# Tables of LayerNorm and spatial mixing loaded and turned at the gate, and a longer booking for transposing DMAs in a planned decoder-trunk step

## The chip, the cores and the metric

The kernel runs on one core of one Trainium2 chip. The metric is the device time of one execution in microseconds (us), lower is better. Several executions are timed without the profiler; one more is profiled, and its trace is what the readings below rest on.

## The reference

One layer of a decoder trunk is applied to 1024 prompt rows and 8 sample rows of width 1024, in float32. What matters for this change is the branch A:

```
xn = rmsnorm(h) * pre_g
u, v, z_a, x_b, z_b, g_a, g_b = split(xn @ w_in)          # seven blocks of 1024 columns
u = gelu(u)
vn = layernorm(gelu(v)) * ln_g + ln_b                     # statistics over the 1024 columns of a row
s = tril(w_s[g]) @ vn + b_s[g]                            # 8 groups g of 128 channels, chunks of 128 rows
y_a = u * s * silu(z_a)
...                                                       # branch B: trailing means, block-diagonal product
m = sigmoid(g_a) * (y_a @ w_pa) + sigmoid(g_b) * (y_b @ w_pb)
h = h + rmsnorm(m @ w_out) * post_g
h = h + rmsnorm(sigmoid(rmsnorm(h) @ w_pg) * (p @ w_ple)) * ple_out_g
```

Outputs are the new rows, the normalised v of the last chunk and of the sample rows, and the pooling buffers.

## The kernel before, in words

Float32 accuracy comes from cutting each operand into a high and a low part (`split`: one copy on ScalarE, one subtraction on VectorE) and multiplying three of the four combinations on TensorE. Each block of 1024 output columns is done as four pairs of 128-column tiles. The first pair of v is done classically in four products; every other pair is done after Strassen's scheme in seven products P1, P6, P2, P7, P4, P5, P3 (`strassen`, L632), whose operand quarters of x (B11 to B22, T1 to T4) stay in SBUF, and whose weight combinations (A11, S2, ...) are made on VectorE and cut on both engines a few products ahead. P5 and P3 use one PSUM region: VectorE copies P5's result out before P3 adds to it.

The stream of steps (`run_stream`, L730) goes through v, then the gate g_a, then u and z_a, then branch B, the gate g_b, and the merging products. The raw weights of a pair are asked for six steps ahead (FETCH, L750), and cut three ahead (AHEAD, L32). Work beside the products is hung on steps: `at(step, f)` calls f after that step. A finished pair of v, which has channels on the partitions, is turned to rows: `v_planes` (L871) copies its 16-bit halves to words on ScalarE and has SyncE's queue issue one transposing DMA for each of the two tiles, `v_join` (L880) copies the turned halves to their place on ScalarE, and `v_turn` (L889) applies gelu there. The 8 sample rows of v are turned on TensorE. In the gate's first products the LayerNorm of the rows follows (`ln_stats`, `ln_apply` L917), first that of the samples, whose rows are multiplied and shifted by the tables `lng` and `lnb`; `sample_spatial` (L1001) is their mixing, `spatial_offsets` (L965) and `spatial` that of the prompt.

The tables of the change: `ln_loads` (L936) loads w_s (0.5 MB) and 16 short rows of ln_g and ln_b; `spatial_weights` (L948) masks w_s on GpSimd, turns it in eight 128 by 128 transposes on TensorE, cuts it in two `split`s into the tiles `wst`, and turns the 16 short rows into `lncol`; `ln_rows` (L943) loads ln_g, ln_b and b_s broadcast to all partitions, 0.5 MB each.

The order of instructions is not that of the code. A planner (class `Planner`) records every operation with its engine, its estimated duration, the tiles it touches, and its due time `at`: the time of the TensorE stream at which it was asked for. It then simulates the five engines and emits each engine's instructions in the order of their planned start (`order`, L202). Latest starts are counted back from TensorE's due times (`wanted`, L180). An operation is planned no earlier than 14 us ahead of its latest start or its `at`, whichever comes first (`LOAD`, `LEAD`, L65). Among operations that an engine could start at the same time the one with the earliest latest start goes first; an engine waits for one that is overdue and soon ready, when the other can spare the time (L248). A DMA keeps its queue busy for `op.busy`, then shares one pipe of 0.36 MB per us for `op.moved`, and lands `op.lands` later. Nearly all tiles live in 46 equal slots (SLOTS, L31) that are handed on in the order in which they come free; a load is planned only when three more slots than it needs are free (`SPARE`, L65). On the chip each engine, and SyncE's queue among them, works through its instructions in the planned order, and a semaphore makes it wait where data is later than planned.

```
161:        if method[:9] == "dma_start":
162:            op.busy, op.moved = 1.0 if engine == "gpsimd" else 0.45, writes[0].size() * (2e-6 if writes[0].dtype == U16 else 4e-6)
163:            op.lands = 4.5 if kwargs.get("accum_op") is not None else 2.0
...
1278:    at(c[1], ln_loads)
1279:    at(vsteps[1][2], spatial_weights)
...
1289:    at(vsteps[3][0], ln_rows)
```

`c` is the classical first pair of v, `vsteps[i]` the steps of v's pair i, `gasteps[0]` those of the gate's first pair.

Of the kernel before, what the change touches and what calls it, by code (L numbers as in the profile page):

```python
# [55 lines left out]
class Planner:  # L56
# [89 lines left out]
    def take(self, engine, method, args, kwargs):  # L146
        given = [*(("out" if i == 0 else "", a) for i, a in enumerate(args)), *kwargs.items()]
        writes = [a for k, a in given if k in ("out", "accum_out") and a is not None]
        reads = [a for k, a in given if k not in ("out", "accum_out") and hasattr(a, "tensor")]
        if kwargs.get("accum_op") is not None:  # L150
            reads += writes
        name = writes[0].tensor.name
        if engine == "tensor" and self.open is not None and self.open[0] == name:
            op = self.open[1]
        else:
            op = Op(engine, len(self.ops), self.clock, self.fixed)
            self.ops.append(op)
        self.open = (name, op) if engine == "tensor" else None
        op.calls.append((method, args, kwargs))
        op.spent.append(op.busy)  # L160
        if method[:9] == "dma_start":
            op.busy, op.moved = 1.0 if engine == "gpsimd" else 0.45, writes[0].size() * (2e-6 if writes[0].dtype == U16 else 4e-6)
            op.lands = 4.5 if kwargs.get("accum_op") is not None else 2.0
        else:
            took = self.duration(engine, method, writes[0], reads, kwargs)
            op.busy += took
            if engine == "tensor" and not self.fixed:
                self.clock += took
            if engine == "scalar":
                op.table = self.TABLES.get(kwargs["func"], 0)  # L170
        for ap in reads:
            self.touch(op, ap, False)
        for ap in writes:
            self.touch(op, ap, True)
# [124 lines left out]
@with_exitstack  # L299
def tile_hybrid_step(ctx, tc, *args):  # L300
    hybrid_step(ctx, tc, *args)


def hybrid_step(
# [107 lines left out]
    class Operand:  # L412
# [37 lines left out]
        def at(self, what, k):  # L450
            return [part[:, k % 2, :] for part in self.parts[what, k // 2]]
# [437 lines left out]
    def v_turn(out, pair, ts):  # L889

        if ts == [S]:
            ps = bank("vt")
            for m in range(2):
                nc.tensor.transpose(ps[:NS, m * P : (m + 1) * P], out[m][:, SEQ:T], ident)
        for t in ts:
            n, c = rows(t), slice(2 * pair * P, (2 * pair + 2) * P)
            v = vtok(t)[:n, c]
            nc.scalar.activation(out=v, in_=ps[:NS, : 2 * P] if t == S else v, func=AF.Gelu_apprx_tanh,
                                 accum_out=vsums[:n, t, pair : pair + 1])
# [324 lines left out]
    def pairs_of(c0, cls, key):  # L1224
        return [(Weights(inp(c0, i), key), cls(i, key)) for i in range(NPAIR)]
# [5 lines left out]
    vsteps, vusers = [], []  # L1231
# [3 lines left out]
    gasteps = [strassen(w, xop, u) for w, u in pairs_of(GA0, Gate, "ga")]  # L1235
# [11 lines left out]
    flat, c = big.rearrange("p b t -> p (b t)"), [T + 4 * w for w in (0, HALF, HALF + WIDE, HALF + 2 * WIDE)]  # L1247
# [20 lines left out]
    c = vsteps[0]  # L1268
# [6 lines left out]
    at(vsteps[1][0], lambda: xop.cut("T4"))  # L1275


    at(c[1], ln_loads)
    at(vsteps[1][2], spatial_weights)
    for i, u in enumerate(vusers):  # L1280

        nxt = vsteps[1][1:] + vsteps[2] if i == 0 else (vsteps[i + 1] if i + 1 < NPAIR else gasteps[0])
# [3 lines left out]
            at(nxt[2 + m], lambda u=u, i=i, m=m: v_join(u.out, i, m))  # L1286
        for s, ts in zip(nxt[4:], V.turns):
            at(s, lambda i=i, ts=ts: v_turn(None, i, ts))
    at(vsteps[3][0], ln_rows)
    flow = [s for p in gasteps for s in p] + [s for p in usteps[0] for s in p]  # L1290
    for n, t in enumerate([NB - 1, *range(NB - 1)]):
        s = 5 + 4 * n
# [43 lines left out]
    p, l, c = gbsteps[2], gbsteps[3], pasteps[0]  # L1336
    turn_over(yaop, l, [*l[1:], c[0]])
    p, l, c = pasteps[2], pasteps[3], pbsteps[0]
# [196 lines left out]
    l, c = pbsteps[3], outsteps[0]  # L1535
    turn_over(woop, l, [*l[2:], c[0], c[1]], ("B11", "T3", "T2", "B21", "T4", "T1", "B22"))
    l, c = outsteps[3], gatesteps[0]
# [194 lines left out]
```

## Time and profile before

| | us |
|---|---|
| median of 3 runs | 1000.1 (1000.04 to 1001.04) |
| profiled execution, whole | 997.51 |
| its span, first to last instruction | 995.8 |
| PE (TensorE matmul) busy | 981.3 |
| DVE (VectorE) busy | 800.5 |
| ACT (ScalarE) busy | 526.0 |
| POOL (GpSimd) busy | 72.7 |

The span is what the profile shows from the first to the last instruction; the execution's time has 1.7 us more around it. Busy times of different engines overlap. PE stands for matmuls and PEld for weight loads; SP is SyncE, which only issues DMAs here. Tiles go by the program's names: `vw` is a cut weight or the words of v, `garaw` the gate's raw weights, `gas` their sums, `gaw` their cut parts, `v<-vw` on SP a transposing DMA, `big<-v` on ACT the copy of turned halves, `vt` the turned sample rows of v, `acc` a PSUM region, `u` a Strassen partial sum. A timeline row gives start, length, engine, line, operation, tiles, shapes and count, and in brackets the idle time of the engine before it and what ended it. All operations are recorded by the planner, so they share one line, L297, and are told apart by tiles.

### The profile page before, as it was taken

The page shows a single profiled execution, that of the slowest core. Times are in us where ns is not written, and L with a number is a line of the kernel's source. Part 1 is how long each engine was busy: PE and PEld are TensorE (multiplying, and loading weights), DVE is VectorE, ACT ScalarE, POOL GpSimd, SP SyncE. Part 2 cuts the span into 40 slices and gives each one's busy share as a digit, 9 for nine tenths or more (in the row PEclk, how much of TensorE's full clock was granted, in tenths as well). Part 3 has the DMA queues.
Part 4 walks back from the last instruction along what each step waited for, and adds up shares of the span by engine and source line. Part 5 has one row for each costly group of instructions (what it writes and reads, how often), then busy time and mean ns, then how long its engine had stood idle before and what let it go on. Part 6 is the DMA issues. An engine that isn't in the chain of part 4 may idle for free. (4 is left out here: it accounts for less than half of the span.)

```text
span 995.8 us, 16069 instructions
## 1 busy us (share of the span) xinstructions
PE 981.3 (99%) x6136; PEld 881.0 (88%) x6136; DVE 800.5 (80%) x1241; ACT 526.0 (53%) x925; POOL 72.7 (7%) x162
## 2 busy tenths in 40 slices
PE   8999999999999999999999999999999999999996
PEld 6889989999999899999999999999999988888885
DVE  5975468777778888888897987697799798779796
ACT  7767888756434434243433343562353365677653
POOL 2200000000000000001000100000000002312111
PEclk9999999999999999999999999999999999999999
DMA  9334462232365355546635166874663553389646
GB/s 342 128 124 85 110 169 106 86 107 64 135 230 186 104 184 185 197 134 227 240 120 166 40 238 232 287 287 149 215 254 110 172 206 68 84 275 364 166 108 191
DMA packets 103970, 171.14 MB, mean 172 GB/s; under 512 B 24254, under 2 KB 64238, under 8 KB 103885
## 3 DMA queue, kind: packets, MB, share of 16 engines
q1 hardware_dynamic: 101525, 162.21, 47.9%
q0 software_dynamic: 2048, 7.37, 4.3%
q8 instruction: 48, 0.79, 0.3%
q10 hardware_dynamic: 320, 0.54, 0.2%
q14 instruction: 29, 0.24, 0.1%
HBM read 114.59 MB, written 51.77 MB: 167 GB/s over the span
## 5 line engine op out<-in xcount | busy, mean ns | idle before, releaser
L297 DVE TENSOR_TENSOR u<-acc,u 128x520 f32<-128x520 f32 (+1 forms) x90 | 62.6, 696 | 38.8 <-PE acc L297 36.8
L297 POOL TENSOR_TENSOR rstd<-ms,mhalf 128x1 f32<-128x1 f32 (+1 forms) x45 | 36.5, 812 | 213.6 <-DVE ms L297 213.5
L297 POOL MEMSET u<- 128x8 f32 x35 | 3.5, 105 | 558.1 <-PE acc L297 310.9
L297 ACT ACTIVATE u<-acc 128x512 f32<-128x512 f32 x39 | 23.2, 595 | 26.9 <-PE acc L297 26.4
L297 ACT ACTIVATE paw<-pas 128x512 fp32r<-128x512 f32 x16 | 10.1, 629 | 31.2 <-DVE pas L297 25.9
L297 ACT ACTIVATE pbw<-pbs 128x512 fp32r<-128x512 f32 x16 | 10.0, 630 | 28.2 <-DVE pbs L297 24.9
L297 DVE TENSOR_TENSOR big<-big 128x1024 f32<-128x1024 f32 (+4 forms) x20 | 23.6, 1217 | 0.0
L297 ACT ACTIVATE big<-v 128x1024 uint16<-128x1024 uint16 x16 | 18.5, 1173 | 8.4 <-DMA v<-vw 8.4
L297 ACT ACT_TABLE_LOAD x15 | 19.2, 1283 | 6.5 <-PE acc L297 5.5
L297 ACT ACTIVATE big<-pht,gvec 128x128 f32<-128x128 f32 x64 | 18.0, 381 | 8.1 <-PE pht L297 8.1
L297 ACT ACTIVATE big<-mix 128x256 f32<-128x256 f32 x32 | 12.2, 384 | 16.9 <-PE mix L297 16.2
L297 PE MATMUL accm<-qh,wpoolw 128*128 128x260 f32 (+1 forms) x96 | 20.9, 320 | 0.0
L297 DVE TENSOR_TENSOR acc<-acc,u 128x512 f32<-128x512 f32 (+1 forms) x16 | 11.2, 699 | 8.8 <-PE acc L297 8.8
L297 DVE TENSOR_TENSOR big<-mix,big 128x256 f32<-128x256 f32 x32 | 13.2, 422 | 5.9 <-ACT big L297 5.0
L297 ACT ACTIVATE zbw<-zbs 128x512 fp32r<-128x512 f32 x16 | 10.1, 632 | 14.6 <-DVE zbs L297 7.2
L297 ACT ACTIVATE zaw<-zas 128x512 fp32r<-128x512 f32 x16 | 10.0, 630 | 14.5 <-DVE zas L297 9.0
L297 ACT ACTIVATE gbw<-gbs 128x512 fp32r<-128x512 f32 x16 | 10.0, 626 | 13.9 <-DVE gbs L297 12.0
L297 PEld LDWEIGHTS accm<-qh,wpoolw 128*128 128x128 f32 x96 | 15.5, 188 | 1.9
L297 ACT ACTIVATE zbw<-zbraw 128x512 fp32r<-128x512 f32 x12 | 7.5, 627 | 17.8 <-DMA zbraw<-in_w_in_dram 16.3
L297 ACT ACTIVATE uw<-us 128x512 fp32r<-128x512 f32 x16 | 10.0, 627 | 12.3 <-DVE us L297 9.8
L297 ACT ACTIVATE junk<-ge 128x512 bf16<-128x512 f32 (+2 forms) x19 | 11.6, 609 | 8.9 <-DVE ge L297 8.3
L297 ACT ACTIVATE gb<-gb 128x1032 f32<-128x1032 f32 (+1 forms) x8 | 6.8, 854 | 17.6 <-DVE gb L297 17.6
(689 smaller groups left out, 3632.2 us busy)
## 6 DMA issues: line engine op xcount, KB each, us to landing
ga<-ga SPq DMA_DIRECT2D x16, 516.0 KB
gb<-gb SPq DMA_DIRECT2D x16, 516.0 KB
ya<-za SPq DMA_DIRECT2D x8, 516.0 KB
yb<-zb SPq DMA_DIRECT2D x8, 516.0 KB
x<-in_x_prompt_dram SPq DMA_DIRECT2D x8, 512.0 KB
vraw<-in_w_in_dram SPq DMA_DIRECT2D x8, 512.0 KB
e<-e SPq DMA_DIRECT2D x8, 512.0 KB
garaw<-in_w_in_dram SPq DMA_DIRECT2D x8, 512.0 KB
```

What stands on the lines that cost most here:

```text
L297: getattr(getattr(self.nc, e), method)(*args, **kwargs)
```

## The change

A transposing DMA gets costs of its own in the planner: it keeps its queue for 3.0 us, takes almost nothing of the pipe, and lands 1.5 us later. The loads of w_s and of the short rows are asked for after the fourth product of v's third pair instead of after the second product of all; the turning of these tables, and the broadcast rows of ln_g, ln_b and b_s, after the first product of the gate instead of after the third product of v's second pair and the first product of v's fourth. The functions themselves are unchanged.

```diff
@@ -161,6 +161,8 @@
         if method[:9] == "dma_start":
             op.busy, op.moved = 1.0 if engine == "gpsimd" else 0.45, writes[0].size() * (2e-6 if writes[0].dtype == U16 else 4e-6)
             op.lands = 4.5 if kwargs.get("accum_op") is not None else 2.0
+            if method == "dma_start_transpose":
+                op.busy, op.moved, op.lands = 3.0, 0.01, 1.5
         else:
             took = self.duration(engine, method, writes[0], reads, kwargs)
             op.busy += took
@@ -1275,8 +1277,8 @@
     at(vsteps[1][0], lambda: xop.cut("T4"))
 
 
-    at(c[1], ln_loads)
-    at(vsteps[1][2], spatial_weights)
+    at(vsteps[2][3], ln_loads)
+    at(gasteps[0][0], spatial_weights)
     for i, u in enumerate(vusers):
 
         nxt = vsteps[1][1:] + vsteps[2] if i == 0 else (vsteps[i + 1] if i + 1 < NPAIR else gasteps[0])
@@ -1286,7 +1288,7 @@
             at(nxt[2 + m], lambda u=u, i=i, m=m: v_join(u.out, i, m))
         for s, ts in zip(nxt[4:], V.turns):
             at(s, lambda i=i, ts=ts: v_turn(None, i, ts))
-    at(vsteps[3][0], ln_rows)
+    at(gasteps[0][0], ln_rows)
     flow = [s for p in gasteps for s in p] + [s for p in usteps[0] for s in p]
     for n, t in enumerate([NB - 1, *range(NB - 1)]):
         s = 5 + 4 * n
```

## The prediction

> **What bounds the kernel now.** I read the busy time by stretches first, because the page gives PE 99% of the span and the question is where the last per cent sits.
>
> ```profile
> core 0 of [0], span 995.8 us
> core 0: us, PE busy (x) PEld busy (x) DVE busy (x) ACT busy (x) POOL busy (x), PEclk, DMA share, GB/s
> 0.00:25.00 25.00, 20.79 (x116) 17.16 (x117) 14.00 (x28) 19.05 (x31) 7.04 (x29) 1.00 0.99 348
> 75.00:100.00 25.00, 25.00 (x173) 22.98 (x172) 14.68 (x24) 18.03 (x27) 0.00 (x0) 1.00 0.48 86
> 125.00:135.00 10.00, 8.14 (x53) 6.80 (x53) 7.79 (x13) 7.96 (x18) 0.00 (x0) 1.00 0.68 199
> 135.00:165.00 30.00, 30.00 (x204) 27.62 (x203) 22.94 (x47) 28.26 (x60) 2.38 (x5) 1.00 0.45 112
> 320.00:330.00 10.00, 9.47 (x68) 8.76 (x67) 9.93 (x17) 5.38 (x11) 0.11 (x1) 1.00 0.17 51
> 980.00:995.80 15.80, 7.87 (x46) 6.72 (x44) 10.02 (x20) 5.86 (x15) 2.42 (x3) 0.87 0.77 233
> sum 995.80, PE 981.27 PEld 880.98 DVE 800.49 ACT 525.97 POOL 72.70; mean PE 98.13 PEld 88.10 DVE 80.05 ACT 52.60 POOL 7.27
> ```
>
> PE is idle for 995.80 − 981.27 = 14.53 us: 4.21 in the start, 7.93 in the tail, 1.86 between 125 and 135, 0.53 between 320 and 330. These four add up to 14.53, so PE has no other idle time. Start and tail lie outside the edits; what can be won lies at 125 to 135, where the last pair of v ends and the gates begin. Second, PE's timeline there (start, length, instruction, idle before it), and at 325.
>
> ```profile
> 124.83 0.40 PE L297 MATMUL acc<-xT1l,vw 128*128 128x260 f32 x2
> 125.07 0.40 PE L297 MATMUL acc<-xT1h,vw 128*128 128x260 f32 x2
> 126.86 0.51 PE L297 MATMUL acc<-xB22h,vw 128*128 128x260 f32 x2 [1.40 <-DVE v L297]
> ...
> 132.42 0.40 PE L297 MATMUL acc<-xB11h,gaw 128*128 128x512 f32 x1
> 132.96 0.38 PE L297 MATMUL vt<-ident,v 128*8 128x128 f32 x2
> ...
> 133.44 0.40 PE L297 MATMUL acc<-xT2l,gaw 128*128 128x260 f32 x2
> 134.16 0.75 PE L297 MATMUL acc<-xT2h,gaw 128*128 128x260 f32 x4 [0.32 <-DVE gaw L297]
> ...
> 325.00 0.50 PE L297 MATMUL acc<-xB11h,zaw 128*128 128x512 f32 x1 [0.53 <-DVE u L297]
> ```
>
> A pair of 260-column matmuls normally takes 0.24 (124.83 to 125.07), also where the printed length is 0.40. So the losses by starts are 126.86 − 125.07 − 0.24 = 1.55, then 132.96 − 132.42 − 0.23 = 0.31 (0.23 for one of 512), then 134.16 − 133.44 − 0.24 = 0.48: 2.34 us in all. The wait at 325 (0.53 by its row) has no edit near it. Third, what kept DVE and ACT, and behind them the load queue, SP.
>
> ```profile
> 125.51 0.69 DVE L297 TENSOR_TENSOR gas<-garaw,garaw 128x512 f32<-128x512 f32 x1 [4.95 <-DMA garaw<-in_w_in_dram]
> 126.12 0.69 DVE L297 TENSOR_TENSOR v<-acc,u 128x520 f32<-128x520 f32 x1
> ...
> 129.08 0.69 DVE L297 TENSOR_TENSOR gaw<-garaw,gaw 128x512 fp32r<-128x512 f32 x1 [1.67 <-ACT gaw L297]
> ...
> 132.21 0.69 DVE L297 TENSOR_TENSOR v<-acc,u 128x520 f32<-128x520 f32 x1
> ...
> 133.42 1.89 DVE L297 TENSOR_TENSOR gaw<-gas,gaw 128x512 fp32r<-128x512 f32 x3
> ```
>
> ```profile
> 127.34 1.19 ACT L297 ACTIVATE big<-v 128x1024 uint16<-128x1024 uint16 x1 [2.01 <-DMA v<-vw]
> 128.43 1.67 ACT L297 ACTIVATE gaw<-garaw 128x512 fp32r<-128x512 f32 x3
> ```
>
> ```profile
> 104.22 1.79 SPq L297 DMA_TRANSPOSE v<-vw  x1
> ...
> 116.72 1.74 SPq L297 DMA_TRANSPOSE v<-vw  x1
> 118.55 1.76 SPq L297 DMA_DIRECT2D garaw<-in_w_in_dram  x2
> 120.41 4.90 SPq L297 DMA_TRANSPOSE v<-vw  x1
> 125.40 0.53 SPq L297 DMA_DIRECT2D lng<-in_ln_g_dram  x1
> ...
> 126.50 0.37 SPq L297 DMA_DIRECT2D bsb<-in_b_s_dram  x1
> ...
> 136.84 1.49 SPq L297 DMA_TRANSPOSE v<-vw  x1
> ...
> 140.27 3.37 SPq L297 DMA_TRANSPOSE v<-vw  x1
> 143.74 0.52 SPq L297 DMA_DIRECT2D garaw<-in_w_in_dram  x1
> ```
>
> A transposing issue holds SP for 1.49 to 4.90 us; the planner books 0.45. The gate's two raw loads stand behind one, so they are there only at 125.51. DVE, which works in order, waits 4.95 us for them with the sum of the gate's weights at its head, while the copy of v that PE needs stands behind it until 126.12. ACT does the same at 127.34: it waits 2.01 for the last turned v, with the gate's split behind it.
>
> **The change, part by part.** No arithmetic is added or removed, so PE's work stays as it is; the time can only come from these waits and from new ones.
>
> *The planner's cost.* A transposing DMA is booked 3.0 us on SP instead of 0.45, then 0.03 instead of 1.46 (0.52/0.36) on the wire, and lands 1.5 instead of 2.0 after that. In the plan, with the first transpose at 0 and the order of the rows at 116.72, the second raw load is issued at 3.9 instead of 1.35, and lands at 3.0 + 0.45 + 2 × 1.46 + 2.0 = 8.4 instead of 0.45 + 3 × 1.46 + 2.0 = 6.8. The trace has 125.51 − 116.72 = 8.8. So the planner now knows within half a microsecond when the sum can run. The copy of v can run at the same moment (its product ended at 125.07 + 0.40 = 125.47), is more urgent, and the planner lets an overdue operation go first. That is worth 126.12 − 125.51 = 0.61 on PE's first wait. What is late next: PE would reach the gate's first product 0.61 earlier than now, at about 129.3, but its weights are ready at 129.08 + 0.69 = 129.77, as ACT's split (128.43) stands behind the wait for the turned v. So if nothing else moves, the gain is about 0.1. If the split also comes ahead of that wait, the 0.61 holds and the 0.31 and 0.48 go with it, as both are DVE's run from 129.08 to 133.42 + 1.89 being late: 1.40. The rest of the first wait, 1.55 − 0.61 = 0.94, is the dependence of one product on the copy of the one before it in the same PSUM region, and goes only if another product is put between. The last transpose itself is booked to land at 8.4 instead of 8.3, where the trace has 127.34 − 116.72 = 10.6: the planner still expects it 2 us early. Costs alone therefore point to the lower end, the other edits may point to the upper one. I take the middle of 0.1 and 1.40, 0.7.
>
> *Tables loaded and turned later.* Two small and one 0.5 MB load go from the start of v to the third pair; the turn goes from the second pair to the first gate product. The turn's share on DVE and ACT:
>
> ```profile
> L297 ACT ACTIVATE wst<-psw x2: 572/586/600, 76.4 to 79.4; 128x512 fp32r<-128x512 f32 x2
> L297 DVE TENSOR_TENSOR wst<-psw,wst x2: 683/688/692, 77.0 to 80.8; 128x512 fp32r<-128x512 f32 x2
> ...
> 82.05 0.17 DVE L297 COPY lncol<-lncol 128x16 f32<-128x16 f32 x1
> ...
> 139.64 1.21 DVE L297 TENSOR_TENSOR sv<-sv,lng 8x1024 f32<-8x1024 f32 x1
> ...
> 148.06 1.95 PE L297 MATMUL smix<-diag,sv 8*128 8x8 f32 x16
> ...
> 158.53 1.08 PE L297 MATMUL rowsum<-wst,ones 128*128 128x512 f32 x4
> ```
>
> That is 2 × 0.61 (DVE's spacing of such operations, 125.51 to 126.12) + 0.17 = 1.4 us of DVE and 2 × 0.59 = 1.2 of ACT. They leave 75 to 100, where DVE has 10.3 us idle and PE none, so nothing is won there. They arrive behind 132.65, where DVE is in its run until 135.3. The first reader is the row sum at 158.53, 25 us later, so the planner can place them behind the gate's splits: I take 0, with 0 to 1.4 as bounds (1.4 if they go ahead of the gate's second weights, which PE already waits for). Between 135 and 165 DVE has 7.1 us idle as cover, ACT 1.7, enough for 1.2. PE's nine transposes and POOL's select move along; POOL is idle in 125 to 135. On SP the three issues meet the idle time between 106.0 (104.22 + 1.79) and 116.72: 0. In slots, the raw table and the vectors now hold two from the third pair on where the two turned tables held two: even after that point, two more before it.
>
> *The LayerNorm rows.* Three loads move from the last v pair's first product to the gate's first. Now they are issued at 125.40 to 126.87, long after the code asks for them. They leave three slots for longer. Their first reader is the sample's LayerNorm; their load may be planned from 14 us before it is due. SP is idle from 126.87 to 136.84, so I take 0.
>
> **The sum.** −0.7 + 0 + 0 on the profiled execution of 997.51 (span 995.8 and 1.7 around it) gives 996.8. The median, 1000.1, lies 2.6 above it; carried over, the forecast is 1000.1 − 0.7 = 999.4, with 1000.0 to 998.7 for the ends 0.1 and 1.40, and 1001.4 with the 1.4 of the tables on top of the lower end.
>
> **The rivals.**
> *All three waits go.* If the freed slots let the gate's raw loads out into SP's 10.7 us of idle time before 116.72, they land some 6 us earlier, the gate's first product fits between the two dependent ones, and 1.55 + 0.31 + 0.48 = 2.34 are won: 997.8. For it: that SP stands idle while loads that are due wait. Against it: from the third pair on the count of slots is even.
> *Nothing changes.* The order around 125 comes out the same, since a dearer transpose moves everything behind it alike: 1000.1. Against it: the raw load's booking moves by 1.6 us.
> *The rows come too late (slower).* Slots are short until the tables are turned, which for a few microseconds hold four at the gate, and a load must leave three free. If the rows are put behind the last transpose and the loads around it, they are issued at 143.74 + 0.52 = 144.26 and land 125.51 − 119.78 = 5.7 later (the second raw load's, issued at 118.55 + 1.76 − 0.53), at 150.0. The sample's product by the first row takes 1.21 (139.64), the sum with the second is of the same size, so the sample's mixing starts at 152.4 instead of 148.06: 4.3 lost, less 0.7: 1003.7. It decides from a landing after 148.06 − 2.4 = 145.6. Against it: 10 us of idle SP ahead.
> *The booking is wrong.* If a transpose held SP no longer than a copy, every load behind it would be planned 2.55 us late, and the gate's weights with it: up to 2.55 more PE wait, 1002.6. The 1.49 to 4.90 against 0.37 to 0.53 of single copies speak against it. The Trainium skill, page Advanced Engine Details and Errata, section X-Bar Transpose (TRN2), states that transposing DMAs are as fast as regular ones; by that the old 0.45 would stand. This trace disagrees as far as the issuing queue goes, and the measurement decides.
>
> **How the numbers follow.** Forecast 0.42, all waits gone 0.24, nothing 0.10, rows too late 0.19, booking wrong 0.05. 0.2% is 2.0 us, about what can be told from no change here. Faster by more than that: 0.22 of the second case and 0.06 of the forecast's upper tail, 0.28. Slower: 0.18 + 0.04 + 0.03 of the forecast with dear tables, 0.25. Within: 0.47. The range goes from 997.2, just under the case of all waits gone, to 1003.2, which leaves out the worse half of late rows; the forecast's own is 998.5 to 1001.4.
>
> **What would show it.** The first step holds if DVE's copy of v stands ahead of the gate's sum and PE's wait near 126 is under 1 us. The tables cost nothing if PE waits for neither the turned tables nor the sample's mixing. The slower case shows as a PE wait at the sample's mixing near 148, with DVE idle for the row. Earlier raw loads, issued well before the transpose of 116.72, would make the forecast too high. A PE wait anywhere after 330 would mean that the new order reaches further than I suppose, and makes it wrong.

## The result, and the profile after

The median went from 1000.1 us (998.3 to 1003.17, 7 runs) to 997.04 us (995.85 to 997.32, 7 runs). The ratio is 0.9964, 95% interval [0.9951, 0.9978]: the kernel became 0.36% faster. A later set of runs of both kernels gave 0.9976 (below). The forecast of 999.4 was too high, and the measured median lies 0.16 us under the range, which began at 997.2.

The profiled executions hardly show it: 997.32 us and a span of 995.6 after, 997.51 and 995.8 before. So the stretches are read one by one. Busy time by stretches of the changed kernel, columns as before (length, then busy time and instructions of each engine, granted clock of PE, DMA share, GB/s):

```profile
core 0 of [0], span 995.6 us
core 0: us, PE busy (x) PEld busy (x) DVE busy (x) ACT busy (x) POOL busy (x), PEclk, DMA share, GB/s
125.00:135.00 10.00, 10.00 (x73) 9.30 (x72) 4.74 (x12) 8.72 (x22) 0.00 (x0) 1.00 0.41 124
135.00:165.00 30.00, 30.00 (x195) 27.44 (x194) 22.21 (x44) 24.47 (x48) 1.94 (x5) 0.94 0.42 118
320.00:330.00 10.00, 8.81 (x61) 7.98 (x60) 9.97 (x16) 5.33 (x10) 0.10 (x1) 1.00 0.18 55
```

Three rows answer to those of before. From 125 to 135 PE is busy for 10.00 where it was busy for 8.14: all three waits are gone. From 135 to 165 it is as busy as before, but the clock column has 0.94 instead of 1.00: something is slower there without a wait. From 320 to 330 it is busy for 8.81 instead of 9.47: the wait that the change does not touch grew. PE's timeline at the end of v shows what took the place of the first wait:

```profile
123.62 0.40 PE L299 MATMUL acc<-xT1h,vw 128*128 128x260 f32 x2
123.85 0.39 PE L299 MATMUL acc<-xB11h,gaw 128*128 128x512 f32 x1
...
126.38 0.39 PE L299 MATMUL acc<-xB11h,gaw 128*128 128x512 f32 x1
126.61 0.41 PE L299 MATMUL acc<-xB22h,vw 128*128 128x260 f32 x2
...
129.48 1.04 PE L299 MATMUL psw<-ident,ws 128*128 128x128 f32 x8
130.27 0.49 PE L299 MATMUL acc<-xT2h,gaw 128*128 128x260 f32 x2
...
324.43 0.50 PE L299 MATMUL acc<-xB11h,zaw 128*128 128x512 f32 x1 [1.19 <-DVE u L299]
```

The last product of v's fourth pair, P3 (operand B22), needs VectorE's copy of P5 (operand T1) out of the same PSUM region. Before, P3 came directly behind P5. Now the gate's first product (operand B11, weights `gaw`) fills the 2.76 us between 123.85 and 126.61, and the copy is made meanwhile. That needs the gate's first weights cut before P5 is done, and SP's timeline shows why they are:

```profile
98.72 0.80 SPq L299 DMA_DIRECT2D ws<-in_w_s_dram  x1
...
106.78 0.94 SPq L299 DMA_DIRECT2D garaw<-in_w_in_dram  x2
112.88 4.34 SPq L299 DMA_TRANSPOSE v<-vw  x2
125.98 0.35 SPq L299 DMA_DIRECT2D lng<-in_ln_g_dram  x1
...
134.79 0.52 SPq L299 DMA_DIRECT2D garaw<-in_w_in_dram  x1
135.85 3.25 SPq L299 DMA_TRANSPOSE v<-vw  x1
139.16 0.56 SPq L299 DMA_DIRECT2D garaw<-in_w_in_dram  x1
```

The gate's first two raw loads are issued at 106.78, ahead of v's transposes. Before they were issued at 118.55, between two of them. ScalarE's first split of them runs at 111.30, where it was at 128.43 before; VectorE's first sum of them runs without a wait, and its copy for P3 has nothing in front of it:

```profile
111.30 0.62 ACT L299 ACTIVATE gaw<-garaw 128x512 fp32r<-128x512 f32 x1
```

```profile
113.18 0.68 DVE L299 TENSOR_TENSOR gas<-garaw,garaw 128x512 f32<-128x512 f32 x1
...
124.05 0.70 DVE L299 TENSOR_TENSOR v<-acc,u 128x520 f32<-128x520 f32 x1 [0.99 <-PE acc L299]
```

That is worth about 2.6 us in these two profiles. Why the two profiled executions differ by 0.2 all the same is the matter of the clock column. In windows of 3.41 us:

```profile
141.62:145.03 3.41, 3.41 (x27) 3.23 (x26) 2.83 (x5) 2.56 (x3) 0.00 (x0) 1.00 0.27 86
145.03:148.45 3.42, 3.42 (x24) 3.09 (x23) 2.09 (x7) 3.42 (x8) 0.10 (x1) 1.00 0.25 77
148.45:151.86 3.41, 3.41 (x11) 2.77 (x11) 2.15 (x6) 2.25 (x6) 0.57 (x1) 0.50 0.22 77
151.86:155.27 3.41, 3.41 (x31) 3.41 (x30) 0.78 (x2) 2.31 (x7) 0.00 (x0) 1.00 0.00 0
```

From 148.45 to 151.86 PE was granted half its clock; it did 11 instructions where it does 24 to 31 otherwise. No such stretch was in the profile of before.

To compare profiles I add up PE's losses by starts: for each matmul the distance to the next start, less the median distance of its shape in the changed kernel's profile. A shape's median is not exact, so small negative sums, and differences of some 0.1, mean nothing. By this sum, in us:

| stretch | before | before, second profile | after | after, second profile |
|---|---|---|---|---|
| 0 to 25 | 5.08 | 5.04 | 4.89 | 6.43 |
| 113 to 137 | 2.75 | 3.83 | 0.14 | 0.20 |
| 137 to 170 | -0.09 | 1.72 | 1.47 | -0.10 |
| 320 to 330 | 0.75 | 0.65 | 1.58 | 0.71 |
| last matmul's start to the end | 8.21 | 8.25 | 8.59 | 8.31 |
| span | 995.8 | 998.4 | 995.6 | 994.4 |

The first pair of profiles compares a lucky execution of before with an unlucky one of after: 2.61 won at 113 to 137, then 1.56 lost at 137 to 170, 0.83 at 320 and 0.38 at the end. The second pair has 3.63 won at 113 to 137 and 1.82 at 137 to 170, with 1.39 lost in the start.

### The profile page after: what moved, and what is told of

It is laid out like the page before. It is cut to its first block, busy times and chain, and to the rows that moved or that the text cites. A ratio compares the mean times of both kernels' runs of the same rounds, so it can differ in the third digit from the quotient of the medians.

```text
span 995.6 us, 16051 instructions
## 1 busy us (share of the span) xinstructions
PE 982.1 (99%) x6136; PEld 882.0 (89%) x6136; DVE 799.8 (80%) x1241; ACT 523.0 (53%) x923; POOL 72.8 (7%) x162
## 5 line engine op out<-in xcount | busy, mean ns | idle before, releaser
L299 DVE TENSOR_TENSOR v<-acc,u 128x520 f32<-128x520 f32 (+1 forms) x9 | 6.3, 697 | 14.5 <-PE acc L299 14.4
L299 ACT ACTIVATE vw<-v 128x1024 uint16<-128x1024 uint16 x16 | 16.1, 1045 | 0.5 <-DVE v L299 0.5
```

What stands on the lines that cost most here:

```text
L299: getattr(getattr(self.nc, e), method)(*args, **kwargs)
```

## The experiments

### The two kernels once more

> The kernel before, profiled once more. Its first profiled execution took 997.51 us where the median is 1000.1; the gain of 3.1 us is larger than the 2.34 us of PE waits that the first profile shows at 125 to 135. Theory J (the waits are longer in most executions): this profile shows the same order, PE waits of 4 to 5 us in sum at 125 to 135, and 999 to 1001 us. Theory K (the clock): the waits are again 2.3 us, and a stretch of a few us at a granted clock of 0.5 lies somewhere before the tail, as the changed kernel has one at 148.45 to 151.86; 999 to 1001 us. If it is 997.5 again with neither, both theories stay open.

> The changed kernel, profiled once more. Theory J: no PE wait at 125 to 135 and 995.8 to 997.3 us whatever the clock does. Theory K: the stretch at half clock near 148 is there again (the seven granted clocks of its runs are all 0.996 or 0.997, and 0.998 would be the tail alone), so it belongs to the order of work and not to chance; its cost is 6 matmuls of 512 columns by 0.2 us, 1.2 us.

Measured: before 1000.02 us (998.33 to 1002.21), ratio 1.0005 [0.9991, 1.002]; after 996.39 (995.29 to 998.67), ratio 0.9976 [0.9963, 0.9989]. The second profile of before has the same waits, longer, and one more:

```profile
114.68 0.38 PE L297 MATMUL vt<-ident,v 128*8 128x128 f32 x2 [0.73 <-DVE v L297]
...
128.05 0.51 PE L297 MATMUL acc<-xB22h,vw 128*128 128x260 f32 x2 [1.68 <-DVE v L297]
```

The second profile of before has something of both theories: longer waits (3.83 by starts, where theory J had 4 to 5) and a stretch at half clock. The second profile of after has no wait at 125 to 135, as theory J says, and no stretch at half clock near 148, so theory K's step that the stretch belongs to the order of work falls.

What follows: the waits of the kernel before differ between its two profiles, and the execution that the prediction was worked out from was one of its better ones. The two sets of runs of the same kernel in this comparison, 1000.02 here (10 runs) and 999.04 beside it (30 runs), also show how far a median can be off.

### Each part alone

The booking alone:

```diff
+            if method == "dma_start_transpose":
+                op.busy, op.moved, op.lands = 3.0, 0.01, 1.5
```

> The kernel before with the booking of transposing DMAs alone. Theory S (slots): the gate's raw loads are still issued behind the transpose near 116.7, as the turned tables keep their two slots; PE still waits 1.5 to 2.3 us at 125 to 135; 999 to 1000.5 us. Theory C (cost): the booking alone brings the gate's raw loads out before 110, no PE wait is left there, 996.5 to 997.5 us.

The three moves alone, with the old booking:

> The kernel before with the three moved calls alone and the old booking. Theory S: the raw loads of v and of the gate come out earlier, the gate's before 110, the gate's first product stands between the last two of v, PE waits under 0.5 us at 125 to 135; 996.5 to 997.7 us. Theory C: the raw loads stay behind the transpose near 116.7, PE waits 1.5 us or more; 999 to 1000.5 us.

The tables alone (`ln_loads` and `spatial_weights` moved, `ln_rows` where it was):

> The kernel before with the loads and the turn of the spatial tables moved, and neither the rows nor the booking. Theory S (it is the slots that the two turned tables no longer hold in the second and third pair of v): the first pair's second tile is turned near 78 instead of 92, the gate's raw loads are issued near 108, no PE wait over 0.3 us at 114 to 136; the same as all three moves, 996 to 997.5 us. Rival R (the three broadcast rows held the slots that the gate's loads lacked): the raw loads stay behind the transpose near 117, waits of 2.3 to 3.4 us remain, 999 to 1000.5 us.

The rows alone:

```diff
-    at(vsteps[3][0], ln_rows)
+    at(gasteps[0][0], ln_rows)
```

> The kernel before with the three broadcast rows moved alone. Theory S: the gate's raw loads are issued behind the transpose near 117 to 119 as before, PE waits of 2.3 to 3.4 us at 114 to 136 remain, 999 to 1000.5 us, and nothing is lost at the sample's mixing near 148. Rival R: raw loads before 112, waits gone, 996 to 997.5 us.

Only the longer hold of SP, with the old pipe time and landing:

```diff
+            if method == "dma_start_transpose":
+                op.busy = 3.0
```

> The kernel before with the transposing DMA booked for 3.0 us on its queue and nothing else of the booking (0.52 MB on the pipe and landing 2.0 as before). Theory H (what helps is that the planner knows how long the queue is held, as the prediction's first step has it): DVE's copy of v goes ahead of the gate's sum, waits of under 1 us at 114 to 136, 996 to 997.5 us. Rival W (what helps is that transposes no longer take the pipe, so that the slots which they free are handed on sooner in the plan): one of the gate's raw loads stays behind the transposes near 118, waits of 2 us or more remain there, 998.5 to 1001 us.

| kernel | median us | ratio to before | first two `garaw` issued at | losses 113 to 137 | losses 137 to 170 |
|---|---|---|---|---|---|
| before | 1000.1 | 1 | 118.55 | 2.75 (second profile 3.83) | -0.09 (1.72) |
| after | 997.04 | 0.9964 [0.9951, 0.9978] | 106.78 | 0.14 | 1.47 |
| booking alone | 995.89 | 0.9968 [0.9955, 0.998] | 113.32 | 0.17 | -0.21 |
| all moves alone | 997.03 | 0.9977 [0.9962, 0.9991] | 108.16 | 0.23 | 1.38 |
| tables alone | 997.57 | 0.9981 [0.9965, 0.9996] | 108.21 | 0.22 | 1.37 |
| rows alone | 1001.07 | 1.0018 [1.0004, 1.0032] | 118.45 | 0.15 | 5.30 |
| longer hold alone | 996.0 | 0.9965 [0.995, 0.9979] | 103.20 and 118.66 | 0.10 | 0.28 |

Each ratio is to the runs of the kernel before that were taken beside the kernel in question. Their median was 1000.1 for the changed kernel, 999.04 for the booking and the moves and 998.95 for the other three, so the medians of different rows can be compared only to about 1 us.

The waits at 113 to 137 go in every one of them, by any single part, and the gains do not add. The rows alone contradict both of their theories, since the loads stay behind the transpose and the waits go all the same; with the longer hold alone one load does stay near 118, as theory W has it, but its waits do not come, and VectorE's copy (125.78) goes ahead of the gate's sum (126.39), as theory H has it. With the rows alone the copy stands behind two sums, at 126.53, and PE loses nothing either, so it is not the place of the copy that removes the waits. Without the moves the booking does as much as the whole change, and without the booking the moves do nearly as much. Two of the cases tell why. SP's timeline with the longer hold alone:

```profile
103.20 0.46 SPq L299 DMA_DIRECT2D garaw<-in_w_in_dram  x1
117.05 1.52 SPq L299 DMA_TRANSPOSE v<-vw  x1
118.66 1.26 SPq L299 DMA_DIRECT2D garaw<-in_w_in_dram  x1
```

One early load is enough, as the first product needs the split of only one. Why a longer hold lets this load out so early in the plan was not followed up. And with the rows alone, where both loads stay behind a transpose:

```profile
118.45 1.76 SPq L297 DMA_DIRECT2D garaw<-in_w_in_dram  x2
...
138.00 1.24 SPq L297 DMA_DIRECT2D garaw<-in_w_in_dram  x1
139.33 4.13 SPq L297 DMA_TRANSPOSE v<-vw  x1
143.57 0.52 SPq L297 DMA_DIRECT2D garaw<-in_w_in_dram  x1
```

```profile
125.37 0.39 PE L297 MATMUL acc<-xB11h,gaw 128*128 128x512 f32 x1
...
128.16 0.40 PE L297 MATMUL acc<-xB22h,vw 128*128 128x260 f32 x2
...
151.48 0.77 PE L297 MATMUL acc<-xB22h,gaw 128*128 128x260 f32 x2 [3.34 <-DVE ga L297]
```

```profile
148.51 0.69 DVE L297 TENSOR_TENSOR gas<-garaw,garaw 128x512 f32<-128x512 f32 x1 [4.61 <-DMA garaw<-in_w_in_dram]
...
150.64 0.69 DVE L297 TENSOR_TENSOR ga<-acc,u 128x520 f32<-128x520 f32 x1
```

The raw loads are as late as before, and still the gate's first product stands between P5 and P3, because ScalarE's first split of the gate runs at 123.90 and not at 128.43. The plan says why (planned times of the kernel's own planner, not of the chip). In the plan of before the gate's raw data is there at 122.49, but `lng`, `lnb` and `bsb` are planned at 121.33, 121.78 and 122.46 and take three slots, and ScalarE's first split of the gate, which needs a slot, is planned only at 126.75; the product is ready at 128.51, after P5's planned end at 126.29, and P3 goes first. With the rows alone the split is planned at 123.59, the product is ready at 125.07, and it goes first. In the plans of the other cases it is ready between 120.6 and 121.6. So the plan of before missed this order by 2.2 us, and each part alone gains more than that.

The rows alone also show a trap one pair later. The next pair's raw loads, planned behind transposes that were thought short, are issued at 138.00 and 143.57. VectorE waits 4.61 us for them with the gate's own copy behind, PE waits 3.34, and the kernel is slower than before as a whole. The late loads are not enough for that: before they were issued at 138.39 and 143.74, but VectorE had the copy (148.17) ahead of the sum (150.79), and PE lost nothing there. Nor is the old booking enough: with all three moves and the old booking they are issued at 136.66 and 141.48, and PE has no such wait either. In the changed kernel it is 134.79 and 139.16.

### Fewer slots

The changed kernel with `SLOTS` 44 instead of 46.

> The changed kernel with 44 slots instead of 46. Theory S: this takes back the two slots that the moved tables left; the gate's raw loads go behind the transpose near 115 to 119 again, and PE waits of 1.5 to 4 us come back at 114 to 136: 998 to 1001 us. Rival: if two slots do not matter, the raw loads stay near 107 and the time at 996 to 997.3 us.

Measured: 1025.71 us, ratio 1.0255 [1.0219, 1.0291]. At 113 to 137 nothing is lost (0.23), although the raw loads are issued at 114.47 and 119.60. PE's waits by releaser (total, times, longest) show that the time goes in branch B and the merging products instead:

```profile
PE accm L299 <- ACT wpoolw L299: 6.6, 3, 4.7
PE acc L299 <- ACT xbw L299: 2.4, 1, 2.4
PE acc L299 <- ACT paw L299: 2.0, 1, 2.0
```

What follows: two slots are worth 29 us elsewhere, so this kernel's time tells nothing about the waits of the change. Theory S falls in the waits all the same: the loads are late again, and the order came out well without early loads.

### The order undone, and the order forced

The booking alone, with the gate's first product kept behind P3 by a dependence in the planner:

```diff
+    def gate_last():
+        held, run_p3, run_p1 = [], vsteps[3][6].run, gasteps[0][0].run
+        def p3():
+            run_p3()
+            held.append(plan.ops[-1])
+        def p1():
+            run_p1()
+            plan.ops[-1].before.add(held[0])
+        vsteps[3][6].run, gasteps[0][0].run = p3, p1
+    gate_last()
```

> The booking alone, with one thing undone: the gate's first product may not be emitted before P3 of v's last pair. Order theory (what was won is the gate's first product standing between P5 and P3 of v, which share a PSUM region): PE waits again before P3, 1.5 to 2.0 us, while the smaller waits behind it stay away because the gate's weights are cut in time; 995.9 + 1.5 to 2.0 = 997.4 to 997.9, and at most 999.3 if the smaller ones come back too. Rival (earlier raw loads and a shorter run of VectorE are what count, not the order): waits at 120 to 136 of under 0.5 in all, 995.9 to 996.4.

The kernel before, with P4 put between P5 and P3 in v's last pair:

```diff
+        vsteps.append(strassen(w, xop, u, order=["P1", "P6", "P2", "P7", "P5", "P4", "P3"]) if i == 3
+                      else (strassen if i else classical)(w, xop, u))
```

> The kernel before, with no line of the change; v's last pair alone does its products in the order P1, P6, P2, P7, P5, P4, P3, so that P4 stands between the two that share a PSUM region. Order theory: the wait before P3 (1.55 and 1.84 in the two profiles of before) goes, the gate's weights come no earlier than before and 0 to 0.8 of the waits behind it may stay: 1000.0 less 1.6 to 3.4 = 996.6 to 998.4. Rival (the gate's late raw loads are the cause): the waits only move behind P3, 999.5 to 1000.5.

Measured: with the gate's product kept behind, 999.08 us, ratio 0.9998 [0.9989, 1.0008]: nothing is left of the booking's 0.32%. With P4 between, 999.3, ratio 0.9999 [0.9987, 1.0011]: nothing is won. Of the first, PE's and VectorE's timeline:

```profile
128.01 0.51 PE L299 MATMUL acc<-xB22h,vw 128*128 128x260 f32 x2 [0.79 <-DVE v L299]
```

```profile
127.26 0.70 DVE L299 TENSOR_TENSOR v<-acc,u 128x520 f32<-128x520 f32 x1 [0.39 <-PE acc L299]
```

The copy comes as soon as P5 is done, and P3 still loses 0.95 by starts: that is the bare dependence. Of the second, PE's and ScalarE's:

```profile
129.38 0.50 PE L297 MATMUL acc<-xB11h,gaw 128*128 128x512 f32 x1 [0.92 <-ACT gaw L297]
```

```profile
127.63 1.18 ACT L297 ACTIVATE big<-v 128x1024 uint16<-128x1024 uint16 x1 [2.43 <-DMA v<-vw]
128.72 1.14 ACT L297 ACTIVATE gaw<-garaw 128x512 fp32r<-128x512 f32 x2
```

P3 waits for nothing, but the gate's split stands on ScalarE behind a wait of 2.43 us for the turned v, as before, and PE now waits behind P3. So both theories held for one half each. Losses at 113 to 137, in us, with those of the kernels with the mixing in two groups (below). Early means that ScalarE's first split of the gate runs at 111.30 to 123.90, late that it runs at 128.43 to 129.53:

| | gate's weights late | gate's weights early |
|---|---|---|
| P3 directly behind P5 | 2.75 and 3.83 (before), 3.54 (mixing in two groups) | 1.26 and 1.26 (gate's product kept behind) |
| a product between | 1.58 and 1.47 (P4) | 0.10 to 0.23 (the others) |

Each alone takes away 1.2 us or more, early weights the most, and only both together leave nearly nothing. The order of the changed kernel is both at once: the gate's product can stand between only if its weights are early. Yet 1.26 of loss does not explain the 3.0 us that the median lost. In this profile there were two stretches at half clock, at 10.97 and at 150.92.

### The half clock behind the sample's mixing

A stretch at half clock came at about 148 to 156 in some profiles and not in others. It lasted 3.41 us, or twice that with the rows alone, and in each profile all its edges lie whole multiples of 3.413 us apart, the one in the tail included. Counted from there, the stretch before it held all 16 matmuls of `smix`, 8 columns each and 1.95 us together, in each of the five profiles so far that had it (the second of before, after, all moves, tables, rows). In the five others (the first of before, the second of after, booking, longer hold, 44 slots) an edge fell into the 1.95 us. The gate's product kept behind and P4 between are two more that had it. In six of these seven PE was busy for the whole of that window; with the rows alone it was also idle for 0.79 us of it. In the first profile of after the mixing is this row, in the window from 145.03 to 148.45 above:

```profile
145.12 1.95 PE L299 MATMUL smix<-diag,sv 8*128 8x8 f32 x16
```

Two kernels test it: the changed kernel with the mixing in two groups of 8, one product apart (`sample_spatial` takes a list of heads, at first the first four, each group is an operation of its own in the planner, and the sum on VectorE comes with the second group), and with the 16 matmuls issued twice, the second pass writing the same values.

```diff
     at(flow[6], sample_spatial)
+    at(flow[7], lambda: sample_spatial(range(4, NB)))
```

> The changed kernel, with the sample's mixing issued as two groups of 8 matmuls one product apart instead of one of 16. Theory of the small matmuls (half the clock follows when the 1.95 us of 8-column matmuls fall whole into one stretch of 3.41 us): no stretch at half clock between 140 and 165, wherever the stretches begin; 0.4 of the executions were hit and lost some 1.3, so the median falls by 0 to 0.6 from 996.4 to 997.0: 995.8 to 997.0, too little for the time alone to tell. Rival (the half clock falls where it likes or follows from the loads): a stretch at 145 to 155 as in four of nine earlier profiles.

```diff
-        for h in range(NB):
+        for h in (*range(NB), *range(NB)):
```

> The changed kernel, with the 16 small matmuls of the sample's mixing issued twice in a row (the second pass writes the same values again). Theory of the small matmuls: 3.9 us of them fill at least 1.95 of some stretch of 3.41 us wherever it begins, so the half clock follows in every execution, for 3.4 or 6.8 us: 996.7 plus 1.95 of work plus 0.8 (1.4 in place of 0.4 times 1.3) = 999.4, 998.8 to 1000.8. Rival (no connection): 996.7 plus 1.95 = 998.6, 998.0 to 998.9, with a stretch at half clock there or not.

Windows of the profile with the mixing in two groups (at 145.12 and 151.92), and then with the mixing twice (from 145.53 to 149.26):

```profile
146.03:149.44 3.41, 3.41 (x18) 2.88 (x18) 2.66 (x7) 3.41 (x5) 0.10 (x1) 1.00 0.00 0
149.44:152.86 3.42, 3.42 (x30) 3.29 (x28) 2.88 (x5) 3.42 (x10) 0.57 (x1) 1.00 0.00 0
152.86:156.27 3.41, 3.41 (x28) 3.35 (x28) 2.64 (x7) 3.26 (x8) 0.00 (x0) 1.00 0.00 0
```

```profile
142.83:146.24 3.41, 3.41 (x31) 3.28 (x29) 3.21 (x5) 3.22 (x5) 0.10 (x1) 1.00 0.03 11
146.24:149.66 3.42, 3.42 (x30) 3.35 (x30) 1.66 (x6) 2.71 (x4) 0.00 (x0) 1.00 0.39 145
149.66:153.07 3.41, 3.41 (x10) 2.64 (x9) 1.70 (x4) 1.45 (x3) 0.57 (x1) 0.50 0.02 8
```

No half clock in the first, and one stretch in the second, right behind the window that holds 25 of the 32 small matmuls (3.02 us). The expectation's four of nine earlier profiles should be five of ten, as counted above. The times: 996.6 us, ratio 0.9976 [0.9964, 0.9987], with the mixing split, not to be told from the changed kernel; 999.27, ratio 0.9995 [0.9983, 1.0007], with the mixing twice, close to the 999.4 that the theory expected, though the rival's 998.6 lies inside the spread of its runs (998.1 to 1000.58). The profiles bear the theory out, the times alone would not. What exactly the clock goes by, the number of small matmuls or the work that PE does in a window, is not shown.

### The times without that half clock

With the mixing split in all of them, the cells of the table above should differ by their waits alone.

> The booking alone, with the sample's mixing in two groups one product apart, so that no stretch at half clock can follow from it. No PE wait over 0.3 at 113 to 137, no half clock at 137 to 170. The booking alone had 995.9; less 0 to 0.6: 995.3 to 996.0. It is the measure for the next three.

> The booking alone with the gate's first product kept behind P3, and the mixing in two groups. Theory of two causes (1.1 of its 3.0 was the wait, the rest the half clock at the mixing, which this kernel's mixing hit more often): a wait of 0.9 to 1.3 at 113 to 137, no half clock at 137 to 170, and 0.9 to 1.6 more than the booking with the split mixing: 996.4 to 997.6. Rival (the order alone is worth all of it, in some way that the waits do not show): 2.5 to 3.3 more, 998.2 to 999.2.

> The kernel before with P4 between P5 and P3 of v's last pair, and the mixing in two groups. Theory (the gate's weights are as late as before, and PE waits for them behind P3 instead): 1.2 to 1.6 of waits at 113 to 137 and up to 0.8 more at 160 to 166, so 1.2 to 2.4 more than the booking with the split mixing: 996.8 to 998.4. Rival (separating the two products is worth nothing at all): as the kernel before with the split mixing.

> The kernel before with the mixing in two groups. Theory: all its waits at 113 to 137 (2.75 and 3.83 in the two profiles), no half clock at 137 to 170: 2.6 to 3.7 more than the booking with the split mixing, 998.0 to 999.4, that is 0.2 to 1.0 under the kernel before of the same call. Rival (half clock and mixing have nothing to do with each other): as the kernel before, within 0.3.

| kernel, mixing split | median us | ratio to before | losses 113 to 137 | losses 137 to 170 |
|---|---|---|---|---|
| booking alone | 996.77 (5 runs) | 0.9963 [0.9951, 0.9976] | 0.16 | 0.15 |
| booking, gate's product behind P3 | 996.89 (7 runs) | 0.9969 [0.9958, 0.9981] | 1.26 | 0.11 |
| before | 998.84 (11 runs) | 0.9988 [0.9975, 1.0001] | 3.54 | 0.28 |
| before, P4 between | 1003.04 (11 runs) | 1.0026 [1.0012, 1.0039] | 1.47 | 4.89 |

The kernel with the gate's product kept behind P3, which had lost all of the gain, has it back once the mixing is split: the rival of the two causes (2.5 to 3.3 us above the booking) falls. The 2.2 us from 999.08 to 996.89 are somewhat more than a stretch at half clock cost in the profiles (1.6 to 1.8, below), and the two medians come from different sets of runs, so the size is not exact. The mean granted clocks of the runs fit it: 0.995 or less in nine of twelve runs with the mixing in one group, in three of seven with it split. The 1.1 us of wait between the first two rows did not show in the time, where 0.9 to 1.6 were expected: the booking with the split mixing lost 0.71 at 181.84, in the prompt's mixing, and came out over what I had expected for it, and with 5 and 7 runs the two intervals overlap. So the order by itself, with the weights early in both, is shown by the waits alone. Between the second and third row, where the weights come early and the order stays, the time has 1.95 us and the losses 2.28, which agree.

The fourth kernel missed its forecast of 996.8 to 998.4. With P4 between and the mixing split, the prompt's mixing waits for VectorE's offsets, and two windows at half clock follow from 156.75 on. The window before them, from 153.33, held the second group of 8 small matmuls (1.05 us) and 0.84 us of this wait, so splitting the mixing does not keep half clock away when a wait falls into the same window:

```profile
157.44 0.55 PE L297 MATMUL mix<-wst,vh 128*128 128x256 f32 x1 [1.53 <-DVE off L297]
```

Why the offsets are later there was not followed up, and so no time was measured for a product between with late weights and without half clock. No kernel of this study is better than the changed one by more than the runs can tell: the booking alone, the longer hold alone and the booking with the split mixing lie at 0.9963 to 0.9968, the changed kernel at 0.9964 and 0.9976.

## Why the prediction was wrong

**The likeliest case was the wrong one.** The prediction named the mechanism that came true as a rival, all three waits gone, with the trigger seen in the trace (the gate's raw loads in SP's idle time, its first product between the two dependent ones), and gave it 0.24. The case that it put first, VectorE's copy ahead of the gate's sum, did not occur in the changed kernel, where there is no wait for the sum any more.

**The step that failed is "So if nothing else moves".** The costs were followed along one order of instructions, as the rows of before show it, and the prediction asked how far a shift of 1.6 us goes in it. The question should have been how near the plan was to another order. It was 2.2 us away in the plan, and each part of the change tips it, as does the longer hold out of the booking. "Costs alone therefore point to the lower end" is refuted by the booking alone: 0.9968, no waits.

**"From the third pair on the count of slots is even"** was the argument against the rival, and it counted slots, not when they come free. The tables alone bring the raw loads from 118.55 to 108.21.

**The rows at 0.** "They leave three slots for longer ... I take 0" passed over the one thing that held the gate's first split in the plan of before: these three slots. The rows alone remove all the waits at 113 to 137 (and lose more behind them).

**The tables at 0** were right. PE turns them at 129.48 to 130.27, directly behind P3, and VectorE's and ScalarE's share of it delays no product.

**What is late next:** the 0.94 that was put down to the bare dependence of P3 on the copy was right: 0.95 with the gate's product kept behind and the copy unhindered.

**The size of the rival** is not settled. It had 2.34 us won, 997.8; the medians moved by 3.1 in the first set of runs (ratio 0.9964) and by 2.65 in the second (0.9976). The 2.34 is a sum over one execution of before. Its second profile has 3.42 by the same sum, and the half clock behind the mixing besides. That also weakens the step in which the 2.6 us between the profiled execution and the median were carried over as a constant: in the second profile, 2.6 us longer, they are longer waits and half clock, and the waits go with the change.

**The slower rival** did not occur in the changed kernel, but its kind did with the rows alone: a load planned behind transposes came late, VectorE idled 4.61 us for it, and PE lost 3.34. The late load was the gate's raw weights and not the rows. Neither the changed kernel nor the three moves with the old booking have that wait, so moving the tables as well is enough to avoid it.

**The booking** was right in its direction: a longer hold alone gains 0.35%, though not for the reason that was priced. VectorE's copy does go ahead of the sum there, but with one raw load out at 103.20 the gate's product already stands between, and the copy's place is worth nothing. On the cost of a transposing DMA the Trainium skill, page Advanced Engine Details and Errata, section X-Bar Transpose (TRN2), has transposing DMAs as fast as regular ones. The trace differs as far as the issuing queue goes: in the changed kernel two transposing issues held SP for 4.34 us (at 112.88) and two plain ones for 0.94 (at 106.78).

**The wait at 325** grew from 0.53 to 1.19 in the first profile of after, and was 0.46 in the second. I take it for chance; no run was made on it.

## What to carry to other kernels

In a kernel whose order comes from a planner, an edit is to be costed by how near the plan is to another order, not by how far it shifts the present one: here each of the three parts of the change removed the same waits of some 3 us, and their gains did not add. Two dependent products are best kept apart by one whose weights are certain to be early. With the half clock out of the way, early weights alone won the 1.95 us of the table above; a product between with late weights won nothing that the times could show, and the waits only moved. Before a sum is made from a profiled execution, it should be known what distinguishes it from the median one.

## What the hardware showed beside it

In this kernel half clock followed small matmuls without any idle time of PE in six of seven cases. In each of 12 profiles with the mixing as one group of 16, edges counted in steps of 3.413 us told whether a half-clock stretch followed it: it did in the seven where the 1.95 us fell whole into one window, and it did not in the five where an edge divided them (the most in one window was then 1.83). Beside a profile of the same kernel without it, such a stretch cost 1.6 us (after) and 1.8 (before) by starts.

A second place is the start. In a window of the second profile of after PE is busy for 1.74 of 3.41 us, and the next one runs at half clock:

```profile
8.14:11.55 3.41, 1.74 (x6) 1.24 (x7) 3.15 (x4) 3.41 (x6) 0.00 (x0) 1.00 1.02 414
11.55:14.96 3.41, 3.41 (x9) 2.34 (x8) 2.48 (x8) 3.41 (x7) 2.37 (x4) 0.50 1.03 391
```

In the profiles with this stretch the start lost 6.4 to 6.8 us, in the others 4.9 to 5.4. The Trainium skill, page TensorE: Matmul & The Clock Gate, section "What's actually happening", describes a free-running window of 3413 ns, and the edges here agree with it. The Trainium skill's table in the same section has the half clock come after at least one idle window of some 3.4 us; that covers neither place, since PE had no idle time in the windows of the six cases and 1.7 us of it in the window at the start.

The spread of a kernel's times goes with these windows. Of 113 later runs of the kernel before, 99 had a mean granted clock of 0.995 to 0.998, and their mean times were 997.8 us at 0.998 (27 runs), 998.9 at 0.997 (30), 999.8 at 0.996 (22) and 1001.2 at 0.995 (20). The profiled execution that the prediction rested on was one at 0.998.
